# The gates of the last five tiles of the last unit, projected behind all projections

## The chip, the core and the metric

One NeuronCore of one Trainium2 chip runs the whole program in one launch. The metric is the device time in microseconds, the median over runs; the profile is one execution taken by the hardware profiler. TensorE multiplies (PE in the rows; its weight loads are PEld), VectorE is DVE, ScalarE is ACT, GpSimd is POOL, and SyncE (SP) issues the DMAs from one queue, in order.

## What is computed

One layer of a streaming encoder: 2048 prompt rows of 1024 columns and 8 running streams of 16 new rows each with 512 cached keys. A row is normalised, modulated, projected to queries, keys, values, a SiLU path and gates, goes through two attention branches, and is merged:

```python
h, gate = adaln_modulate(xp, c_prompt, norm_g[l], w_ada[l], b_ada[l])
qa, ka, va, za, qb, kb, vb, zb, ga, gb = project_inputs(h, w_in[l], pos_p)   # h @ w_in, split
...
log_1m = jnp.where(mask, jax.nn.log_sigmoid(-z), 0.0)                        # stick-breaking branch
log_a = jax.nn.log_sigmoid(z) + lax.cumsum(log_1m, axis=3, reverse=True) - log_1m
a = jnp.where(mask, jnp.exp(log_a), 0.0)
...
ya = (oa.reshape(b, s, WIDTH_A) * jax.nn.silu(za)) @ w_branch_a
yb = (ob.reshape(b, s, WIDTH_B) * jax.nn.silu(zb)) @ w_branch_b
return (jax.nn.sigmoid(ga) * ya + jax.nn.sigmoid(gb) * yb) @ w_out
```

The change touches `ga` and `gb`, the 2048 gate columns: they are a part of `h @ w_in` that no attention needs, only the merge at the end.

## The kernel before

**Tiles and units.** The prompt is cut into 16 tiles of 128 rows (t = 0 to 15), the 8 x 16 sample rows are tile 16 (`NT`). The attention is cut into 8 units: units 0, 2, 4, 6 are a head of the differential branch, units 1, 3, 5, 7 two heads of the stick-breaking branch. `steps` is the list of all (unit, tile), the sample tile first in each unit: 136 steps.

**Projection.** `project` makes 12 pieces for a step: 24 matmuls of 128x512 (three products of halves in f16 over eight k) into a PSUM bank `ps_mm`, and in the twelfth piece `finish`, which scales and splits queries, keys and values. Its left operand is the tile of h, 512 KB, which `fetch_h` loads into one of three buffers `hs` (L437), a step ahead. In units 1, 3, 5 and 7, 12 gate pieces follow, two matmuls each (L536), with the unit's 512 gate columns; they go into the single bank `ps_t`, which transposes of queries and keys use too. The last one has ScalarE scale the bank into `gt` (L539), and SyncE stores that to `g_d` in DRAM (L540).

**Attention of unit 7.** For a tile t and each of two heads, chunks of 512 keys: two score matmuls into one of three banks `ps_s` (L696, L697, and L700 with a mask for the diagonal chunk, which comes first), two sigmoids on ScalarE (L130), a scan on VectorE (L670) into `sc_n`. When a segment of up to 8 blocks is scanned, GpSimd multiplies (L676), ScalarE rounds to f16 (L604), VectorE takes the rest (L607), and SyncE transposes both halves by DMA into `wt` (L614). After a lag TensorE sums values with these weights (L757, L758), a pair of matmuls for each half and block.

**Order.** The list `line` holds all projection pieces in order of steps. In turn n of the main loop the attention of step n is interleaved with as many pieces as bring `line` to `position(len(steps) * past / whole + LEAD)`, that is about five steps ahead, by estimated durations. When `line` is used up, the remaining turns take pieces of `early_work` instead: the last of the branch weights, `rest` (buffers for the gates' rows), and the first two tiles of the output stage, whose inputs o and z go into the `hs` buffers 0 and 1 and whose u goes into 2. A scheduler then places every engine's instructions by its own estimates of time; those passed to `kept` stay in program order among each other.

**Output stage.** For each tile: loads of o, z and gate rows, sigmoids, halves of u into `hs` 2 (L314), transposes (L1280), branch matmuls (L1463), transposes of y, output matmuls (L1492); beside it the attention of the sample tile, whose cached keys and values (`dks`, `dc`) are loaded there.

Of the kernel before, what the change touches and what calls it, by code (L numbers as in the profile page):

```python
# [21 lines left out]
AF = mybir.ActivationFunctionType  # L22
# [6 lines left out]
KT = D // P  # L29
# [4 lines left out]
NT = SEQ // P  # L34
# [23 lines left out]
H_AT = 2  # L58
Q_BUFS = 6
TR_AFTER = 5  # L60
LEAD = 5.0
TILE_TIME = 0.6
SAMPLE_TIME = 0.3

GATES = [(u // 2 * 512, u % 2 * 512) for u in range(8)]
# [55 lines left out]
def layer_kernel(ctx: ExitStack, tc: tile.TileContext, a: dict):  # L121
    nc = tc.nc
    V, S, G, T = nc.vector, nc.scalar, nc.gpsimd, nc.tensor
# [12 lines left out]
    def kept(x):  # L136
        tc.keep_in_program_order(x)
        return x
# [190 lines left out]
    units = [None] * 8  # L329
# [101 lines left out]
    silu_z = {}  # L431
    at_hand, ahead, fetched = {}, {}, []

    def fetch_h(u, t):
        ahead[u, t] = hs[len(fetched) % 3].bitcast(F16).rearrange("p (f k n) -> p f k n", f=2, n=P)
        fetched.append(t)
        load(out=ahead[u, t], in_=hT_d[t // 4][:, t % 4, :, :, :])  # L437

    def project(U, t):

        kind, h, sc, sq = U["kind"], U["h"], U["sc"], U["sq"]
        g, i = t // 4, t % 4
        box = {}
# [13 lines left out]
        def mm(n):  # L457
            hi, wi = ((0, 0), (0, 1), (1, 0))[n % 3]
            k = n // 3
            T.matmul(box["p"], box["h"][:, hi, k, :], U["w"][k][:, wi, :], start=(n == 0), stop=(n == 3 * KT - 1))  # L460

        def piece(n):
            if n == 0:
                start()
            for j in range(2 * n, 2 * n + 2):
                mm(j)
            if n == 11:
                finish()
# [57 lines left out]
        g0, gw = GATES[U["u"]]  # L526
        per = 1024 // gw if gw else 0

        def gate_piece(n):

            if n == 0:
                box["g"] = bank("t")
            for j in range(per * n, per * n + per):
                hi, wi = ((0, 0), (0, 1), (1, 0))[j % 3]
                k = j // 3
                T.matmul(box["g"][:, 0:gw], box["h"][:, hi, k, :], U["wg"][k // per][:, k % per, wi, :], start=(j == 0), stop=(j == 3 * KT - 1))  # L536
            if per * n + per == 3 * KT:
                gt = gts[:, 0:512]
                S.activation(out=gt[:, 0:gw], in_=box["g"][:, 0:gw], func=AF.Identity, scale=sc[:, 6:7])  # L539
                load(out=g_d[t][:, g0 : g0 + gw], in_=gt[:, 0:gw])  # L540

        return [lambda n=n: piece(n) for n in range(12)] + [lambda n=n: gate_piece(n) for n in range(3 * KT // per if gw else 0)]

    def transpose_qk(U, t):
        g, i = t // 4, t % 4
# [417 lines left out]
    steps = [(u, t) for u in range(8) for t in [NT] + list(range(NT))]  # L963
# [12 lines left out]
    def projection(m):  # L976
        u, t = steps[m]
        made = []

        def piece(i):  # L980
            if i == 0:
                begin(u, t)
                made.extend(project(units[u], t))
            if i == H_AT and not at_hand and m + 1 < len(steps) and steps[m + 1] not in ahead:
                fetch_h(*steps[m + 1])
            made[i]()

        return [lambda i=i: piece(i) for i in range(12 + 3 * GATES[u][1] // 128)]

    starts = []  # L990
    for m in range(len(steps)):
        starts.append(len(line))
        for i, fn in enumerate(projection(m)):
            line.append((m, fn))
            if i == TR_AFTER and m > 0:
                line.append((m - 1, lambda m=m: transpose_qk(units[steps[m - 1][0]], steps[m - 1][1])))
# [267 lines left out]
    cuts = None  # L1264
    branch_weights = list(range(8))

    L = {}

    def cut(dst, st, src, k, j, s, n):

# [12 lines left out]
    def inputs(t):  # L1283
# [9 lines left out]
        def gates():  # L1293
            gs = []
            for j in range(2):
                gs.append(L["g"][(2 * len(begun) + j) % 4].rearrange("p (b n) -> p b n", b=2))
                load(out=gs[j], in_=g_d[t].rearrange("p (b n) -> p b n", b=2)[:, :, j * 512 : (j + 1) * 512])
            begun.append(t)
            st.update(g=gs, u=L["u"][len(begun) % 2])

# [65 lines left out]
    def early_work():  # L1366


        free.extend(units[7]["bufs"])

        def first(t):
            if "orms" not in L:
                L["orms"] = rsqrt(osums[:, 0:NT, :].rearrange("p t h -> p (t h)"), 4 * NT, P, con, "orms")
            states[t], stages = inputs(t)
            for stage in stages:
                stage()
            if t == tiles[0]:
                turned(states[t])
                opened(states[t])

        def rest():
            L["g"], L["u"], (L["y"], L["y16"]) = free[0:4], free[4:6], free[6:8]

        return [branch_weight for _ in branch_weights] + [rest] + [lambda t=t: first(t) for t in tiles[0:2]]

    for n in range(len(steps) + 2):
        made, qk, side = [], [], []
        if n < len(steps):
            u, t = steps[n]
            past += duration(t)  # L1390
            if t == (3 if u == 0 else NT) and u < 7:
                back += prepare_unit(u + 1)
            if u == 7 and not back and not spare and not cached and len(branch_weights) > 1:
                side.append((1.0, branch_weight))
            for fn in back[: -(-len(back) // max(1, (W_READY if u else W_READY + 2) - t % NT))]:
                side.append((1.0, back.pop(0)))
            for todo, here in ((spare, norm_at), (cached, keys_at)):
                if todo and here(u, t):
                    left = sum(here(*step) for step in steps[n:])
                    for _ in todo[: -(-len(todo) // left)]:  # L1400
                        side.append((1.0, todo.pop(0)))
            if t < NT:
                qk = scores(units[u], t, made)
        target = position(len(steps) * past / whole + LEAD)
        pieces = take(target, min(n + 1, len(steps) - 1))
        if at[0] == len(line) and not pieces and not spare and not cached:
            if cuts is None:
                cuts = early_work()
            pieces = [(1.0, fn) for fn in cuts[: -(-len(cuts) // (len(steps) + 2 - n))]]
            del cuts[: len(pieces)]  # L1410
            if n == len(steps) + 1:
                while due and due[0][2] == 0.0:
                    due.pop(0)[3]()
                pieces += [(PV_B / PIECE, fn) for _, _, _, fn in due]
                due.clear()
        give(interleaved(pieces, qk, side), (PIECE, CHUNK, 0.0))
# [162 lines left out]
```

## Time and profile before

| what | us |
|---|---|
| median of 3 runs (2241.89 to 2244.5) | 2243.91 |
| the profiled execution | 2241.2 |
| its span, first to last instruction | 2239.4 |
| TensorE busy, share of the span | 2082.9, 93% |
| VectorE busy | 1749.2, 78% |
| ScalarE busy | 1621.5, 72% |
| last gate store of unit 7 issued (L540) | 1717.5 |
| last scan of the attention starts (L670) | 1764.2 |
| first branch matmul (L1463) | 1778.8 |

The page gives an engine's busy time and 40 slices of the span with its busy tenths; the table of windows gives the same for stretches that one chooses, with the mean clock granted to TensorE (PEclk) and the share of time in which the DMA engines were busy. In a row of the timeline stand the start, the duration, engine, line, operation, output<-input and, in brackets, the idle time before it with what ended it. Matmuls are pipelined, so the step from one to the next is read from their starts.

### The profile page before, as it was taken

What the parts mean: (1) busy time and instruction counts of PE and PEld (TensorE: products, weight loads), DVE (VectorE), ACT (ScalarE), POOL (GpSimd) and SP (SyncE); (2) the same over time, 40 slices, a digit from 0 to 9 for tenths busy, and PEclk for the clock granted to TensorE, in tenths of its full rate; (3) what the DMA queues carried; (4) which work ended last, traced back from release to release, by engine and by line L of the source; (5) the groups of instructions that cost most, each with busy time, mean ns of one, the idle gap of its engine ahead of it and who ended that gap; (6) DMA issues with size and microseconds to landing.
All of it is one profiled execution on the core that took longest, in us unless ns stands there. A gap on an engine that the chain in (4) does not pass through costs nothing.

```text
span 2239.4 us, 41736 instructions
## 1 busy us (share of the span) xinstructions
PE 2082.9 (93%) x14752; PEld 1127.2 (50%) x14752; DVE 1749.2 (78%) x3795; ACT 1621.5 (72%) x3228; POOL 704.0 (31%) x610
## 2 busy tenths in 40 slices
PE   5998999999999999999989998999998679999997
PEld 3654555555555555555555554555554334444543
DVE  4657868889886788988778888886688868788863
ACT  3967877789877677988677788866677665766641
POOL 1123014456410443742034365402234412212211
PEclk7999999999999999999999999999998799999999
DMA  9777668889796989979879899666677899999521
GB/s 331 266 238 184 165 152 212 196 221 205 197 247 160 224 201 201 213 205 225 200 197 211 182 234 223 170 157 136 140 157 158 183 259 255 235 255 240 158 101 57
DMA packets 805827, 445.30 MB, mean 199 GB/s; under 512 B 537354, under 2 KB 744506, under 8 KB 805104
## 3 DMA queue, kind: packets, MB, share of 16 engines
q1 hardware_dynamic: 804668, 442.24, 79.6%
q8 instruction: 115, 1.88, 0.3%
q14 instruction: 96, 0.79, 0.1%
q10 hardware_dynamic: 948, 0.39, 0.1%
HBM read 228.82 MB, written 86.02 MB: 141 GB/s over the span
## 4 chain that ended last, share of the span: by engine, by line
PE 31%; DVE 7%; ACT 5%; DMA 5%; issue 3%; POOL 1%; SPq 0%; DVEq 0%; POOLq 0%; ACTq 0%
PE ps_o L1492 7%; PE ps_mm L1463 7%; PE ps_mm L460 5%; PE ps_t L536 5%; DMA wt<-sc_n 2%; DVE sc_n L670 2%; PE ps_s L1280 1%; PE ps_s L697 1%; PE ps_s L696 1%; ACT sc_p L130 1%; POOL sc_p L676 1%; PE ps_o L757 1%; PE ps_t L871 1%; ACT sc_n L130 1%; DVE sc_n L607 1%
## 5 line engine op out<-in xcount | busy, mean ns | idle before, releaser
L676 POOL TENSOR_TENSOR sc_p<-sc_p,sc_n 128x127 f32<-128x127 f32 (+7 forms) x192 | 313.1, 1633 | 668.0 <-DVE sc_n L670 515.5
L460 PEld LDWEIGHTS <-hs 128*128 128x128 f16 x3120 | 292.6, 99 | 315.3 <-issue 6.7
L460 PE MATMUL ps_mm<-wa,hs 128*128 128x512 f16 x1590 | 383.3, 380 | 3.3 <-DMA hs<-hT_d 2.1
L460 PE MATMUL ps_mm<-wb,hs 128*128 128x512 f16 x1530 | 382.3, 381 | 0.2 <-DVE qbuf L495 0.2
L536 PE MATMUL ps_t<-wb,hs 128*128 128x512 f16 x1224 | 291.9, 379 | 3.2 <-DVE qst L564 2.9
L670 DVE TENSOR_TENSOR_SCAN sc_n<-ps_s,sc_n,zero_t 128x512 f32<-128x512 f32 x192 | 245.5, 1279 | 35.5 <-ACT ps_s L130 30.1
L696 PE MATMUL ps_s<-k,qst 128*128 128x512 f16 (+3 forms) x640 | 225.7, 354 | 33.5 <-DVE sc_n L670 24.8
L607 DVE TENSOR_TENSOR sc_n<-sc_p,sc_n 128x128 f16<-128x128 f32 (+7 forms) x192 | 221.9, 1158 | 40.0 <-ACT sc_n L604 39.5
L536 PEld LDWEIGHTS <-hs 128*128 128x128 f16 x1632 | 154.8, 98 | 182.2 <-DVE qst L564 7.3
L130 ACT ACTIVATE sc_p<-ps_s,usc 128x512 f32<-128x512 f32 (+3 forms) x320 | 202.9, 634 | 37.6 <-PE ps_s L697 23.0
L697 PE MATMUL ps_s<-k,qst 128*128 128x512 f16 (+3 forms) x640 | 226.1, 354 | 0.0
L604 ACT CAST sc_n<-sc_p 128x128 f16<-128x128 f32 (+7 forms) x192 | 154.8, 807 | 64.7 <-POOL sc_p L676 64.0
L130 ACT ACTIVATE ps_s<-ps_s,usc 128x512 f32<-128x512 f32 (+3 forms) x320 | 195.1, 610 | 0.0
L1492 PE MATMUL ps_o<-wo,wb 128*128 128x512 f16 x816 | 186.7, 385 | 0.7 <-ACT wb L1281 0.7
L757 PE MATMUL ps_o<-v,wt 128*128 128x128 f16 x1088 | 136.1, 227 | 21.8 <-DMA wt<-sc_n 21.8
L1500 POOL TENSOR_TENSOR x<-m,x 128x512 f32<-128x512 f32 x34 | 49.9, 1467 | 272.6 <-DVE m L1496 164.9
L590 DVE TENSOR_SCALAR_CACHE_REDUCE sc_p<-ps_s,usc 128x512 f32<-128x512 f32 (+3 forms) x160 | 106.3, 665 | 32.5 <-PE ps_s L697 18.6
L757 PEld LDWEIGHTS <-wt 128*128 128x128 f16 x1088 | 103.6, 102 | 50.0 <-DMA wt<-sc_n 27.0
L758 PE MATMUL ps_o<-v,wt 128*128 128x64 f16 x1088 | 128.6, 199 | 0.0
L1492 PEld LDWEIGHTS <-wb 128*128 128x128 f16 x816 | 79.6, 99 | 97.1 <-issue 4.6
L670 DVE TENSOR_TENSOR_SCAN sc_n<-ps_s,zero_t 128x128 f32<-128x128 f32 (+3 forms) x128 | 104.2, 815 | 22.9 <-ACT ps_s L130 22.1
L501 POOL TENSOR_TENSOR rot<-pr,rope 128x256 f32<-128x256 f32 x68 | 56.8, 835 | 203.8 <-ACT pr L474 115.1
(370 smaller groups left out, 4572.2 us busy)
## 6 DMA issues: line engine op xcount, KB each, us to landing
hs<-hT_d SPq DMA_DIRECT2D x130, 512.0 KB, 4.8
g_d<-gt SPq DMA_DIRECT2D x68, 256.0 KB, 3.1
out_dram<-pr SPq DMA_DIRECT2D x204, 64.0 KB, 3.6
wa<-in_w_in_dram SPq DMA_DIRECT2D x34, 256.0 KB, 5.3
o_d<-o SPq DMA_DIRECT2D x136, 64.0 KB, 2.0
wa<-g_d SPq DMA_DIRECT2D x17, 512.0 KB, 4.7
wb<-g_d SPq DMA_DIRECT2D x17, 512.0 KB, 4.8
hs<-o_d SPq DMA_DIRECT2D x17, 512.0 KB, 4.2
```

Of the source, the lines that this page charges most:

```text
L130: i = S.activation(**kw)
L460: T.matmul(box["p"], box["h"][:, hi, k, :], U["w"][k][:, wi, :], start=(n == 0), stop=(n == 3 * KT - 1))
L536: T.matmul(box["g"][:, 0:gw], box["h"][:, hi, k, :], U["wg"][k // per][:, k % per, wi, :], start=(j == 0), stop=(j == 3 * KT - 1))
L604: x = S.copy(out=hi, in_=src)
L607: V.tensor_tensor(out=lo, in0=src, in1=hi, op=ALU.subtract)
L670: V.tensor_tensor_scan(out=dst[:, lo : lo + n][:, ::-1], data0=src[:, 0:n][:, ::-1], data1=zero_t[:, 0:1].to_broadcast([P, n]), initial=fi ...
L676: G.tensor_tensor(out=p[:, 0:m], in0=p[:, 0:m], in1=n[:, 1 : m + 1], op=ALU.mult)
L696: T.matmul(p[:, 0:n], qst[:, c, :], kk[:, c, 0:n], start=True, stop=False)
L697: T.matmul(p[:, 0:n], qst[:, 2 + c, :], kk[:, c, 0:n], start=False, stop=not diag)
L757: T.matmul(po[:, c * P : (c + 1) * P], wt[:, wj, :], vt[:, c, :, :], start=first, stop=False)
L1463: T.matmul(pb, st["u"][:, ui * 8 + br * 4 + k, :], wb[br * 4 + k // 2 * 2 + j][:, wi, k % 2, :], start=(n == 0), stop=(n == 11))
L1492: T.matmul(po, st["y"][:, yi * 8 + k, :], wo[j * 4 + k // 2][:, wi, k % 2, :], start=(n == 0), stop=(n == 3 * KT - 1))
```

## The change

`late` names the five steps of unit 7 with t = 11 to 15. For them `project` keeps the 12 gate pieces aside and `projection` issues the first 12 pieces alone, so `line` is 60 pieces shorter. `late_gates` makes these 60 pieces again, in the order t = 13, 14, 15, 11, 12 (`behind`). When `line` is used up, turns take from `behind` first, spread over the turns up to the last but one, and `early_work` follows. The tiles 13, 14 and 15 of h are the last three that were loaded and are still in the three `hs` buffers; those of 11 and 12 are loaded a second time, into the buffers of 13 and 14 when their gates are done. The first matmul of each piece and the evacuation are `kept`.

```diff
+LATE, LATE_DONE = 5, 1
...
+    def late(u, t):
+        return u == 7 and NT - LATE <= t < NT
...
-                T.matmul(box["g"][:, 0:gw], box["h"][:, hi, k, :], U["wg"][k // per][:, k % per, wi, :], start=(j == 0), stop=(j == 3 * KT - 1))
+                x = T.matmul(box["g"][:, 0:gw], box["h"][:, hi, k, :], U["wg"][k // per][:, k % per, wi, :], start=(j == 0), stop=(j == 3 * KT - 1))
+                if late(U["u"], t) and j == per * n:
+                    kept(x)
...
-        return [lambda n=n: piece(n) for n in range(12)] + [lambda n=n: gate_piece(n) for n in range(3 * KT // per if gw else 0)]
+        U["gates", t] = box, [lambda n=n: gate_piece(n) for n in range(3 * KT // per if gw else 0)]
+        return [lambda n=n: piece(n) for n in range(12)] + ([] if late(U["u"], t) else U.pop(("gates", t))[1])
...
-        return [lambda i=i: piece(i) for i in range(12 + 3 * GATES[u][1] // 128)]
+        return [lambda i=i: piece(i) for i in range(12 + (0 if late(u, t) else 3 * GATES[u][1] // 128))]
+
+    def late_gates(t):
+
+        def piece(i):
+            box, made = units[7]["gates", t]
+            if i == 0:
+                if t < NT - 3:
+                    box["h"] = ahead[8, t]
+            made[i]()
+            if i == len(made) - 1 and t >= NT - 3 and NT - LATE + t - (NT - 3) < NT - 3:
+                fetch_h(8, NT - LATE + t - (NT - 3))
+
+        return [lambda i=i: piece(i) for i in range(3 * GATES[7][1] // 128)]
...
+    behind = [fn for t in list(range(NT - 3, NT)) + list(range(NT - LATE, NT - 3)) for fn in late_gates(t)]
...
-            if cuts is None:
-                cuts = early_work()
-            pieces = [(1.0, fn) for fn in cuts[: -(-len(cuts) // (len(steps) + 2 - n))]]
-            del cuts[: len(pieces)]
+            todo = behind
+            left = max(1, len(steps) - LATE_DONE - n)
+            if not behind:
+                if cuts is None:
+                    cuts = early_work()
+                todo, left = cuts, len(steps) + 2 - n
+            pieces = [(1.0, fn) for fn in todo[: -(-len(todo) // left)]]
+            del todo[: len(pieces)]
```

What becomes of it is seen in the order of the built programs. Line numbers of the changed kernel are higher: L540 is the gate matmul (L536 before), L705 and L706 the scores, L766 and L767 the value sum, L623 the DMA transpose, L441 the load of h, L548 the store of gates.

TensorE at t = 13, before: the last gate (t = 15) ends, the first scores of t = 13 follow (256 columns in `ps_s_21915`), then value sums and scores.

```order
L536 MATMUL ps_t_21835<-wb6_1432,hs0_180 128x512
...
L536 MATMUL ps_t_21835<-wb0_1426,hs0_180 128x512
...
L696 MATMUL ps_s_21915<-k_21461,qst_21630 128x256
...
L757 MATMUL ps_o_21842<-v_20665,wt_21646 128x128
...
L696 MATMUL ps_s_21924<-k_20764,qst_21630 128x512
```

TensorE at the same place in the changed kernel: scores of t = 13 (`ps_s_21768`), value sums, and only then the first late gate, that of t = 13 (`hs1`).

```order
L705 MATMUL ps_s_21768<-k_21395,qst_21519 128x256
...
L705 MATMUL ps_s_21783<-k_20764,qst_21519 128x512
...
L766 MATMUL ps_o_21810<-v_19306,wt_21505 128x128
...
L540 MATMUL ps_t_21765<-wb3_1429,hs1_181 128x512
...
L705 MATMUL ps_s_21799<-k_20082,qst_21519 128x512
...
L540 MATMUL ps_t_21765<-wb0_1426,hs1_181 128x512
```

All five gates now stand between the first scores of t = 13 and the first of t = 15, with the remaining scores of t = 13 and 14 and 138 matmuls of the value sum between them; before, none did.

SyncE in the same part, before: a transpose of t = 12, the last gate store, and loads for the output stage right behind the last of t = 12 (its `wt` has 10 half blocks).

```order
L614 DMA_TRANSPOSE wt_21897<-sc_n_21800 128x10x128
L1297 DMA wb3_1429<-g_d1_97 128x2x512
L1290 DMA hs0_180<-o_d0_62 128x1024
L540 DMA g_d15_111<-gt0_1421 128x512
```

SyncE in the changed kernel: the stores of the late gates, the two reloads of h (`hs1`, `hs2` from `hT_d`) and the first loads of the output stage (o, z, a row of gates) stand between the transposes of t = 13 and 14.

```order
L548 DMA g_d13_109<-gt0_1421 128x512
L441 DMA hs1_181<-hT_d2_59 128x2048
L623 DMA_TRANSPOSE wt_21854<-sc_n_21773 128x12x128
L441 DMA hs2_182<-hT_d3_60 128x2048
...
L1313 DMA hs0_180<-o_d0_62 128x1024
...
L1314 DMA hs1_181<-z_d0_79 128x512
L623 DMA_TRANSPOSE wt_22098<-sc_n_22039 128x16x128
L548 DMA g_d11_107<-gt0_1421 128x512
L1320 DMA wb3_1429<-g_d1_97 128x2x512
```

Each of these loads waits for the gate whose buffer it overwrites, and the transposes that follow it are issued after it.

ScalarE early in the output stage, before (`v16c` is cached values, `dsc` the sample tile's exponentials, `hs2` the halves of u):

```order
L314 ACTIVATE v16c_22923<-dc_22758,s_c_22586 128x8x128
...
L314 ACTIVATE v16c_23051<-dc_22804,s_c_22586 128x8x128
L130 ACT_TABLE_LOAD
L130 ACTIVATE dsc_22865,l_22891<-dsc_22865,nm_22889 128x640
...
L130 ACT_TABLE_LOAD
L130 ACTIVATE hs1_181<-hs1_181 128x512
L314 ACTIVATE hs2_182<-hs0_180,suy_22775 128x1024
```

ScalarE there in the changed kernel:

```order
L315 ACTIVATE wo7_22634<-x_22633,s_w8_19830 128x1024
L131 ACT_TABLE_LOAD
L131 ACTIVATE dsc_22867,l_22893<-dsc_22867,nm_22891 128x640
...
L315 ACTIVATE v16c_23053<-dc_22806,s_c_22588 128x8x128
L1496 CAST wa5_174<-wb3_1429 128x512
L315 ACTIVATE hs2_182<-hs0_180,suy_22777 128x1024
L131 ACT_TABLE_LOAD
L131 ACTIVATE hs1_181<-hs1_181 128x512
```

The table load with the exponentials has moved ahead of the last cached values, and the halves ahead of the second table load; `wo7`, the last of the output weights, stood behind both before. With it, the 48 output matmuls of the first tile (L1492), which stood as 30, 8, 10 with transposes and branch matmuls of the next tiles between, are one row of 48.

More of the change, by code (lines that the diff above doesn't have):

```diff
@@ L535, in gate_piece @@
                 k = j // 3
-                T.matmul(box["g"][:, 0:gw], box["h"][:, hi, k, :], U["wg"][k // per][:, k % per, wi, :], start=(j == 0), stop=(j == 3 * KT - 1))
+                x = T.matmul(box["g"][:, 0:gw], box["h"][:, hi, k, :], U["wg"][k // per][:, k % per, wi, :], start=(j == 0), stop=(j == 3 * KT - 1))
+                if late(U["u"], t) and j == per * n:
+                    kept(x)
             if per * n + per == 3 * KT:
                 gt = gts[:, 0:512]
-                S.activation(out=gt[:, 0:gw], in_=box["g"][:, 0:gw], func=AF.Identity, scale=sc[:, 6:7])
+                x = S.activation(out=gt[:, 0:gw], in_=box["g"][:, 0:gw], func=AF.Identity, scale=sc[:, 6:7])
+                if late(U["u"], t):
+                    kept(x)
                 load(out=g_d[t][:, g0 : g0 + gw], in_=gt[:, 0:gw])
-        return [lambda n=n: piece(n) for n in range(12)] + [lambda n=n: gate_piece(n) for n in range(3 * KT // per if gw else 0)]
+        U["gates", t] = box, [lambda n=n: gate_piece(n) for n in range(3 * KT // per if gw else 0)]
+        return [lambda n=n: piece(n) for n in range(12)] + ([] if late(U["u"], t) else U.pop(("gates", t))[1])
     def transpose_qk(U, t):
```

## The prediction

> **What bounds the kernel now.** I read the page first, for the place where TensorE, nearly full everywhere else, has room:
>
> ```profile
> PE 2082.9 (93%) x14752; PEld 1127.2 (50%) x14752; DVE 1749.2 (78%) x3795; ACT 1621.5 (72%) x3228; POOL 704.0 (31%) x610
> PE   5998999999999999999989998999998679999997
> PEclk7999999999999999999999999999998799999999
> ```
>
> Slices 31 to 33 (about 1680 to 1850 us) are the last attention tiles and the start of the output stage. I cut that part by the table of windows, at the first scan of an attention tile of the last unit (t = 9, 13, 14, 15), at the last scan and at the first branch matmul:
>
> ```profile
> core 0: us, PE busy (x) PEld busy (x) DVE busy (x) ACT busy (x) POOL busy (x), PEclk, DMA share, GB/s
> 1644.10:1716.65 72.55, 72.21 (x514) 38.42 (x512) 57.52 (x85) 55.03 (x109) 25.24 (x20) 1.00 0.75 161
> 1716.65:1731.60 14.95, 9.13 (x76) 5.19 (x75) 14.04 (x20) 12.60 (x24) 9.27 (x6) 0.69 0.67 162
> 1731.60:1748.90 17.30, 11.34 (x75) 6.48 (x75) 16.57 (x18) 13.99 (x24) 10.37 (x5) 0.60 0.67 118
> 1748.90:1765.40 16.50, 7.34 (x73) 4.25 (x72) 16.12 (x17) 12.41 (x19) 10.31 (x5) 0.81 0.71 118
> 1778.80:1827.00 48.20, 36.45 (x208) 16.44 (x208) 35.84 (x77) 27.36 (x35) 10.02 (x7) 0.92 0.99 257
> 1716.65:1765.40 48.75, 27.81 (x222) 15.91 (x220) 46.73 (x53) 39.00 (x64) 29.95 (x16) 0.70 0.68 131
> ```
>
> Up to 1716.65 TensorE is the bound (72.21 of 72.55 us) and VectorE has 15 us to spare. From there to 1765.40 it is the reverse: VectorE 46.73 of 48.75 us (0.958), TensorE 57%, and its granted clock falls to 0.60. So work taken off TensorE in the first stretch is worth something only until VectorE is full there, and what is added in the second costs only what TensorE cannot fit.
>
> **The change, part by part.** It moves 5 gates of 24 matmuls of 128x512. Their price, and that of what stands beside them, is the distance of starts in the timeline of TensorE:
>
> ```profile
> 1709.45 0.22 PE L757 MATMUL ps_o<-v,wt 128*128 128x128 f16 x1
> 1709.54 0.22 PE L757 MATMUL ps_o<-v,wt 128*128 128x128 f16 x1
> 1710.22 1.46 PE L536 MATMUL ps_t<-wa,hs 128*128 128x512 f16 x6
> 1711.52 1.46 PE L536 MATMUL ps_t<-wb,hs 128*128 128x512 f16 x6
> 1714.54 0.27 PE L696 MATMUL ps_s<-k,qst 128*128 128x256 f16 x1
> 1723.62 0.59 PE L696 MATMUL ps_s<-k,qst 128*128 128x512 f16 x1 [1.86 <-DVE sc_n L670]
> 1733.38 0.61 PE L696 MATMUL ps_s<-k,qst 128*128 128x512 f16 x1
> 1733.78 0.63 PE L697 MATMUL ps_s<-k,qst 128*128 128x512 f16 x1
> 1743.79 0.38 PE L696 MATMUL ps_s<-k,qst 128*128 128x512 f16 x1 [0.46 <-DVE sc_n L670]
> ```
>
> Six gate matmuls take 1.30 us, so one 0.216 and 120 of them 25.9 us. A pair of the weighted value sum (L757, L758) takes 0.085 us. At a low clock a 128x512 matmul takes 0.40 us (1733.38 to 1733.78).
>
> *First stretch, t = 9 to 12.* All 120 left from here (in the planner 7, 17, 12 and 24 gate pieces of two matmuls at t = 9 to 12). TensorE's load falls to 72.21 - 25.9 = 46.3 us and VectorE's 57.52 becomes the bound. How full can VectorE get? The second stretch shows 0.958 with TensorE half idle; below stand the two fullest mixed stretches, 0.914 and 0.892, in which TensorE is busy too.
>
> ```profile
> 200.00:300.00 100.00, 86.51 (x629) 49.85 (x628) 80.19 (x219) 76.95 (x175) 7.80 (x9) 0.95 0.67 157
> 500.00:600.00 100.00, 96.30 (x730) 53.36 (x729) 91.37 (x194) 88.39 (x191) 58.70 (x56) 1.00 0.89 207
> 700.00:800.00 100.00, 93.58 (x647) 50.98 (x645) 73.50 (x165) 75.05 (x166) 33.66 (x32) 1.00 0.84 206
> 900.00:1000.00 100.00, 93.14 (x711) 52.21 (x709) 89.21 (x190) 88.09 (x190) 61.28 (x57) 0.98 0.91 210
> ```
>
> 57.52 / 0.958 = 60.0 and 57.52 / 0.892 = 64.5 us are the ends. I take 0.935, between them since TensorE's load will be between those of the rows: 61.5 us, a gain of **11.0** (8.1 to 12.5).
>
> That TensorE will have holes here brings its clock in. At 61% busy the clock was 0.69, at 87% 0.95; 46.3 us at about 0.85 are 54 us, still under 61.5, and this is why I don't take 0.958. [...]
>
> *Second stretch, t = 13 and 14.* In the new order all 120 gate matmuls stand between the first scores of t = 13 and the first of t = 15. Before, this took TensorE 1743.79 - 1714.54 = 29.25 us, with idle time and at the low clock. Now it holds 25.9 us of gates; 12 pairs of 512-column scores, 12 x 2 x 0.216 = 5.2; four shorter pairs with their masks, 1.3; 69 pairs of the value sum, 5.9: 38.3 us at full clock. That exceeds the 32.3 us which VectorE takes for these two tiles (1716.65 to 1748.90), so **TensorE becomes the bound here**. It will be 38.3 of some 41 us busy, 93%, and at 93 to 96% the rows above show a clock of 0.98 to 1.00, so full clock stands. To it come stalls behind the weight transposes. These are what SyncE's rows and TensorE's waits show now:
>
> ```profile
> 1746.30 0.29 PE L757 MATMUL ps_o<-v,wt 128*128 128x128 f16 x1 [1.86 <-DMA wt<-sc_n]
> 1752.02 0.23 PE L757 MATMUL ps_o<-v,wt 128*128 128x128 f16 x1 [1.13 <-DMA wt<-sc_n]
> 1741.23 12.29 SPq L614 DMA_TRANSPOSE wt<-sc_n  x4
> hs<-hT_d SPq DMA_DIRECT2D x130, 512.0 KB, 4.8
> ```
>
> I take 3 us of stalls (two such waits), with 1 and 6 as ends: 41.3 us. The lead of TensorE over the scan matters too:
>
> ```profile
> 1716.65 0.69 DVE L670 TENSOR_TENSOR_SCAN sc_n<-ps_s,zero_t 128x256 f32<-128x256 f32 x1
> 1748.94 1.21 DVE L670 TENSOR_TENSOR_SCAN sc_n<-ps_s,zero_t 128x512 f32<-128x512 f32 x1
> ```
>
> Before, scores led the scan by 2.1 us at t = 13 (TensorE the bound) and 5.15 us at t = 15 (VectorE the bound). Afterwards it should be the other way round, 5.15 and 2.1. So scan to scan the stretch takes 41.3 - 5.15 + 2.1 = 38.3 us instead of 32.3: a loss of **6.0** (4.0 to 9.0).
>
> *Waits that are added.* SyncE's queue now holds the two reloads of h, which wait for the gates of t = 13 and 14, and the first loads of the output stage (o, z and one of the gates' rows), which wait for the gates of t = 15, 11 and 12; the transposes of tiles 13 and 14 queue behind them, and TensorE's value sums wait for those. A reload itself lands in 4.8 us, and between its issue and its use stand two gates (10.4 us) and other matmuls, so it costs nothing unless the queue stands. ScalarE evacuates the five gates here instead of earlier:
>
> ```profile
> L539 ACT ACTIVATE gt<-ps_t,usc x10: 687/687/719, 1596.2 to 1715.2; 128x512 f32<-128x512 f32 x10
> ```
>
> Five times 0.69 is 3.4 us; 39.00 + 3.4 of 38.3 + 16.5 = 54.8 us is no bound. A gate also waits for the evacuation of the one before, since its PSUM bank is single; between two gates stand 1.5 us or more of other matmuls.
>
> *Tile 15 and the end of attention* hold no gate and stay at 16.5 + 13.4 us.
>
> *Output stage.* The scheduler has also reordered its beginning, where TensorE stood 11.75 of 48.20 us:
>
> ```profile
> 1812.11 6.64 PE L1492 MATMUL ps_o<-wo,wb 128*128 128x512 f16 x30
> 1826.03 1.03 PE L1280 MATMUL ps_s<-id,hs 128*128 128x128 f16 x8 [7.28 <-ACT hs L314]
> 1818.29 1.15 ACT L314 ACTIVATE v16c<-dc,s_c 128x1024 f16<-128x1024 f32 x1 [0.52 <-DMA dc<-in_cache_a_v_dram]
> 1819.46 1.28 ACT L130 ACT_TABLE_LOAD   x1
> 1823.01 1.28 ACT L130 ACT_TABLE_LOAD   x1
> 1824.84 1.13 ACT L314 ACTIVATE hs<-hs,suy 128x1024 f16<-128x1024 f32 x1
> ```
>
> In the new order the halves of hs stand ahead of the second table load, and the first load with its two exponentials ahead of the last two v16c: of 6.5 us between 1818.29 and 1824.84 only v16c (1.15) and a short cast stay, so some 4.7 leave the path. And all 48 output matmuls of the tile stand ahead of the stall, not 30, so 18 x 0.216 = 3.9 us more of it is filled. Against it, DMA is 0.99 busy here, and the last load of the output weights now goes ahead of the caches'. Ends: 6 us gained; 4 us lost (one landing more on the path). I take a gain of **1.5**, since saturated DMA will give much of it back.
>
> *Sum*: -11.0 + 6.0 - 1.5 = -6.5 us on a span of 2239.4 (execution 2241.2), so 2232.9 (2234.7). That execution lies 2.7 us under the median of 2243.9; I predict a median of **2237.4 us**. The ends together give -14.5 to +4.9.
>
> **Rivals.** *All hidden (15%)*: VectorE as full as in the second stretch now, 12.5 gained, 4 lost, and the output stage gives 5: 13.5, 2230.4 us. For it: the transposes hardly stopped TensorE in the first stretch. Against: three engines near full at once.
>
> *Given back (25%)*: TensorE's work is only shifted, and with VectorE at 0.90 and 5 us of stalls the tail is 8.6 gained, 8 lost, the output stage nothing: 2243.3 us. For it: the second stretch's load (38.3) exceeds its room.
>
> *The SyncE queue stands (13%, slower)*: the five added waits each hold the transposes behind them some 2.5 us too long (the size of the waits for wt above, 1.13 and 1.86, plus an issue), TensorE halts at the value sums that stand ahead of the next gate, and that gate frees the next load later. 12.5 us of stalls beyond the 3 make it +7.5 in the tail, with nothing from the output stage 2251.4 us. It decides from 8 us of stalls in the second stretch on. Against it: loads were issued between transposes before, too, without such a halt.
>
> *Cold gates (5%, slower)*: if the clock stays where it is now in this stretch, 120 matmuls take 0.40 instead of 0.216 us, 22 us more, some 2259 us. The rows at 93% speak against it.
>
> **Chances.** Forecast 42%. This kernel's measurement tells 0.2% (4.5 us) from no change, so up to 2239.4 is faster: forecast and "all hidden", 57%; "given back" is the same, 25%; slower 18%. Range 2231 to 2246: it leaves out the far end of "all hidden" and the two slower rivals; the forecast's own is 2232 to 2239.
>
> **What would show it.** Right: gates of t = 11 to 15 beside the scores of t = 13 and 14 at 0.216 us each; the first scan of t = 13 about 11 us earlier, that of t = 15 about 5, TensorE over 90% busy between, and VectorE no longer. Wrong: waits for wt of more than 6 us in that stretch; a clock under 0.9 there; a stretch t = 9 to 12 above 65 us; or an output stage that is longer from first branch matmul to the end.

## The result, and the profile after

The changed kernel takes 2237.2 us (median of 22 runs, 2232.59 to 2244.71) against 2243.8 us for the kernel before in the same comparison (22 runs, 2235.05 to 2250.03): a ratio of 0.9971, 95% interval 0.9961 to 0.9981. Two more comparisons on other occasions gave 0.9959 (0.9948 to 0.9971) and 0.9976 (0.9963 to 0.999). So it is some 5 to 9 us faster, 0.3%.

From the page of the changed kernel, the span, the busy times and the 40 slices of TensorE and its clock:

```profile
span 2233.3 us, 41751 instructions
PE 2074.0 (93%) x14752; PEld 1123.6 (50%) x14752; DVE 1749.3 (78%) x3795; ACT 1621.4 (73%) x3228; POOL 699.5 (31%) x610
PE   5998899999999999999999998999898699999997
PEclk7999999999999999999999999999999799999999
```

The dip of slices 31 to 33 before (8, 6 and 7 tenths) has lost its last slice; the share of busy TensorE is 93% as before. For the rest I use the same cuts as the prediction, and name them: **A** from the first scan of t = 9 to the first of t = 13, **B** from there to the first of t = 15, then t = 15 up to the *start* of the last scan, the end of the attention up to the first branch matmul, and the **output stage** to the end of the span. The table of windows of the changed kernel, five rows in this order (length first, then busy time and count of each engine, clock, DMA share):

```profile
core 0: us, PE busy (x) PEld busy (x) DVE busy (x) ACT busy (x) POOL busy (x), PEclk, DMA share, GB/s
1648.50:1706.52 58.02, 50.26 (x399) 28.40 (x398) 53.96 (x85) 52.45 (x106) 24.34 (x19) 0.94 0.83 168
1706.52:1748.93 42.41, 40.23 (x294) 21.34 (x293) 31.83 (x36) 27.48 (x47) 19.66 (x12) 0.97 0.81 186
1748.93:1764.46 15.53, 6.15 (x45) 3.19 (x44) 14.97 (x17) 12.88 (x20) 9.85 (x4) 0.77 0.49 101
1764.46:1779.44 14.98, 7.56 (x80) 6.67 (x81) 9.07 (x26) 7.71 (x12) 5.43 (x5) 0.50 0.97 225
1779.44:2233.30 453.86, 430.62 (x3076) 211.21 (x3076) 338.52 (x762) 260.25 (x355) 86.53 (x62) 0.98 0.74 199
```

The same five of the kernel before:

```profile
1644.13:1716.65 72.52, 72.18 (x513) 38.42 (x512) 57.52 (x85) 55.01 (x109) 25.24 (x20) 1.00 0.75 161
1716.65:1748.94 32.29, 20.51 (x150) 11.70 (x149) 30.65 (x38) 26.63 (x46) 19.64 (x11) 0.64 0.67 138
1748.94:1764.15 15.21, 7.30 (x73) 4.21 (x72) 14.83 (x15) 12.03 (x19) 10.31 (x5) 0.84 0.74 121
1764.15:1778.82 14.67, 7.54 (x80) 6.65 (x81) 9.08 (x26) 8.09 (x13) 5.16 (x5) 0.50 0.95 226
1778.82:2239.40 460.58, 431.89 (x3076) 210.57 (x3076) 336.94 (x762) 260.23 (x355) 89.51 (x62) 0.97 0.73 196
```

A went from 72.5 to 58.0 (-14.5), B from 32.3 to 42.4 (+10.1); the next two grew by 0.3 each; the output stage gave 6.7 in this pair of executions. The roles are swapped as forecast: in A VectorE is now busy 0.93 of the time and TensorE 0.87; in B TensorE is busy 40.23 of 42.41 us. Note that the first scan of t = 9 comes 4.4 us *later* than before: executions of one kernel differ there by more than that (1644.13 and 1654.20 in two profiles of the kernel before). So stretches are compared from this scan on, not spans.

### The profile page after: what moved, and what is told of

Same layout as the page of the kernel before. It is cut to its first block, busy times and chain, and to the rows that moved or that the text cites. A ratio compares the mean times of both kernels' runs of the same rounds, so it can differ in the third digit from the quotient of the medians.

```text
span 2233.3 us, 41751 instructions
## 1 busy us (share of the span) xinstructions
PE 2074.0 (93%) x14752; PEld 1123.6 (50%) x14752; DVE 1749.3 (78%) x3795; ACT 1621.4 (73%) x3228; POOL 699.5 (31%) x610
## 5 line engine op out<-in xcount | busy, mean ns | idle before, releaser
L685 POOL TENSOR_TENSOR sc_p<-sc_p,sc_n 128x127 f32<-128x127 f32 (+7 forms) x192 | 310.7, 1622 | 673.1 <-DVE sc_n L679 526.1
L540 PE MATMUL ps_t<-wb,hs 128*128 128x512 f16 x1224 | 293.3, 380 | 3.5 <-DVE qst L573 2.9
L705 PE MATMUL ps_s<-k,qst 128*128 128x512 f16 (+3 forms) x640 | 223.6, 350 | 34.7 <-DVE sc_n L679 27.4
L616 DVE TENSOR_TENSOR sc_n<-sc_p,sc_n 128x128 f16<-128x128 f32 (+7 forms) x192 | 218.8, 1143 | 42.7 <-ACT sc_n L613 42.2
L540 PEld LDWEIGHTS <-hs 128*128 128x128 f16 x1632 | 154.8, 98 | 182.6 <-DVE qst L573 7.3
L706 PE MATMUL ps_s<-k,qst 128*128 128x512 f16 (+3 forms) x640 | 223.7, 350 | 0.0
L766 PE MATMUL ps_o<-v,wt 128*128 128x128 f16 x1088 | 135.9, 226 | 22.8 <-DMA wt<-sc_n 22.6
L767 PE MATMUL ps_o<-v,wt 128*128 128x64 f16 x1088 | 127.9, 198 | 0.0
L766 PEld LDWEIGHTS <-wt 128*128 128x128 f16 x1088 | 102.4, 101 | 50.7 <-DMA wt<-sc_n 26.8
L505 POOL TENSOR_TENSOR rot<-pr,rope 128x256 f32<-128x256 f32 x68 | 58.2, 856 | 201.3 <-ACT pr L478 131.1
L762 PE MATMUL ps_o<-v,wt 128*128 128x128 f16 x544 | 101.6, 224 | 21.0 <-DMA wt<-sc_n 20.8
```

The lines of the kernel that those rows point to most:

```text
L540: x = T.matmul(box["g"][:, 0:gw], box["h"][:, hi, k, :], U["wg"][k // per][:, k % per, wi, :], start=(j == 0), stop=(j == 3 * KT - 1))
L616: V.tensor_tensor(out=lo, in0=src, in1=hi, op=ALU.subtract)
L685: G.tensor_tensor(out=p[:, 0:m], in0=p[:, 0:m], in1=n[:, 1 : m + 1], op=ALU.mult)
L705: T.matmul(p[:, 0:n], qst[:, c, :], kk[:, c, 0:n], start=True, stop=False)
L706: T.matmul(p[:, 0:n], qst[:, 2 + c, :], kk[:, c, 0:n], start=False, stop=not diag)
L766: T.matmul(po[:, c * P : (c + 1) * P], wt[:, wj, :], vt[:, c, :, :], start=first, stop=False)
```

## Experiments

The table holds every profiled execution. "Late gates" are the recorded gate matmuls of the late tiles in A, B and t = 15 (120 in all, 24 to a tile; some records are double or missing, and with five late tiles the first two start in the last 0.8 us of A); times in us. A dash stands where there is one execution alone, and so no ratio.

| kernel | late gates A, B, t = 15 | A | B | t = 15 | to branch | output stage | ratio to before (95%) |
|---|---|---|---|---|---|---|---|
| before, twice | 120, 0, 0 | 72.5, 72.5 | 32.3, 32.2 | 15.2, 15.2 | 14.7, 15.0 | 460.6, 460.2 | 1 |
| the change, three times | 0, 119, 0 | 58.0, 58.0, 58.0 | 42.4, 42.4, 42.4 | 15.5, 15.5, 15.5 | 15.0, 15.1, 15.1 | 453.9, 459.5, 459.7 | 0.9971, 0.9959, 0.9976 |
| five late, over t = 13 to 15, twice | 0, 71, 48 | 58.1, 58.0 | 34.3, 35.3 | 18.5, 18.2 | 14.1, 14.0 | 460.1, 461.8 | 0.9957 (0.9941 to 0.9974), 0.9967 (0.9953 to 0.9981) |
| four late, over t = 13 and 14 | 24, 76, 22 | 59.7 | 35.5 | 15.7 | 17.3 | 460.2 | 0.9966 (0.9953 to 0.9979) |
| four late, over t = 13 to 15 | 24, 52, 46 | 59.8 | 34.7 | 14.8 | 16.9 | 461.9 | 0.9969 (0.9956 to 0.9981) |
| three late, over t = 13 and 14 | 48, 72, 0 | 61.3 | 41.7 | 14.3 | 15.5 | 461.2 | 0.9994 (0.998 to 1.0008) |
| three late, over t = 13 to 15 | 48, 48, 24 | 61.3 | 37.1 | 13.5 | 16.8 | 463.6 | 0.996 (0.9947 to 0.9973) |
| five late, 23 of 24 matmuls left out | 0, 5, 0 | 58.0 | 32.9 | 16.3 | 15.1 | 462.4 | 0.994 (0.9919 to 0.996) |
| three late, short products | 48, 72, 0 | 61.3 | 37.5 | 11.2 | 17.0 | 464.3 | - |
| the change, short products | 0, 119, 0 | 58.1 | 40.6 | 16.2 | 14.8 | 458.8 | - |

The theory: B's length is set by TensorE, which the gates fill, and A's by VectorE. The rivals: the place of the gates in the order, not their amount; VectorE's own stretched operations; the output stage's new order as the real source of the gain.

**Three late tiles instead of five**, none loaded twice:

```diff
-LATE, LATE_DONE = 5, 1
+LATE, LATE_DONE = 3, 1
```

> Three late tiles in place of five (the gates of t=13, 14 and 15 alone stand behind the projections, all from the h at hand, none loaded twice). The stretches are A (first scan of t=9 to first scan of t=13; 72.5 us before, 58.0 with the change), B (to the first scan of t=15; 32.3 and 42.4) and the output stage (its first matmul to the end; 460.6 and 453.9). Theory T (in B TensorE has become the bound, by the number of gate matmuls put there): 48 matmuls of 0.216 us leave B and come back to A. B's TensorE work falls from 40.2 to about 30 us, under VectorE's 31 to 32, so B is 32 to 35; A's TensorE work rises from 50.3 to about 60.7, so A is 60 to 63; A and B together 93 to 98 against 100.4 with the change and 104.8 before, and the kernel 3 to 7 us faster than with the change if the output stage stays. Rival R (it is not the amount but the order: blocks of up to 24 gates stand ahead of the score matmuls on TensorE and each makes the next scan late by its own length): two blocks less of five, so B falls only by what stood ahead of scores, to 38 or more. Rival O (the gain is the output stage's new order and nothing of the gates): A and B together stay within 3 us of 100.4 or of 104.8, and the time follows the output stage.

Measured: no gain at all (0.9994). A is 61.3 as expected, but B is 41.7, not 32 to 35, although only 72 gates stand in it. The theory in its plain form falls here: TensorE is busy 33.1 of B's 41.7 us. The window row shows who is full instead, VectorE with 37.84:

```profile
1715.75:1757.44 41.69, 33.11 (x254) 18.55 (x252) 37.84 (x39) 30.58 (x52) 20.04 (x11) 0.92 0.75 159
```

Its groups of instructions in B (busy time, mean, and idle time before), the subtraction L616 (in the expectations also called a sum) ahead of all others:

```profile
L616 DVE TENSOR_TENSOR sc_n<-sc_p,sc_n 128x1024 f16<-128x1024 f32 (+3 forms) x9 | 17.0, 1896 | 0.0
L679 DVE TENSOR_TENSOR_SCAN sc_n<-ps_s,sc_n,zero_t 128x512 f32<-128x512 f32 x12 | 15.4, 1280 | 1.0 <-ACT ps_s L131 0.3
L240 DVE TENSOR_SCALAR sc_q<-ps_t 128x8 f32<-128x8 f32 x1 | 0.2, 167 | 2.0 <-PE ps_t L232 2.0
```

The twelve scans of 512 columns take 1.280 us each, against 1.279 in the changed kernel's B and 1.280 in that of before. Nine subtractions take 17.0 us; in the changed kernel nine took 12.6. The timelines of GpSimd and VectorE in this run show how one of them is stretched:

```profile
1739.37 1.77 POOL L685 TENSOR_TENSOR sc_p<-sc_p,sc_n 128x895 f32<-128x895 f32 x1 [2.02 <-DVE sc_n L679]
1739.40 2.82 DVE L616 TENSOR_TENSOR sc_n<-sc_p,sc_n 128x1024 f16<-128x1024 f32 x1
```

and an undisturbed one in the changed kernel:

```profile
1720.43 1.23 DVE L616 TENSOR_TENSOR sc_n<-sc_p,sc_n 128x1024 f16<-128x1024 f32 x1 [2.67 <-ACT sc_n L613]
```

The product ends at 1741.14 and the subtraction, started 0.03 us after it, at 1742.22, 1.08 us after the product's end. The undisturbed one takes 1.23 us in all, so this one got next to nothing done beside the product.

**Five late tiles, spread over three tiles of attention instead of two**:

```diff
-LATE, LATE_DONE = 5, 1
+LATE, LATE_DONE = 5, 0
```

> Five late tiles, but their 60 pieces are spread over the tiles t=13, 14 and 15 instead of 13 and 14, so that about 80 of 120 gate matmuls stand in B and about 40 beside t=15's scans (C, first to last scan of t=15, 15.5 us with the change, of which TensorE works 6.2). Theory T: B's TensorE work falls from 40.2 by about 8.6 us to some 32, so B is 32 to 36; C takes 8.6 us of gates into 9 us of idle TensorE and stays 15 to 18; A is the 58 of the change. The tail is 5 to 9 us shorter than with the change, the kernel 4 to 9 us faster. Rival R (each block of gates makes the score behind it late by its own length, idle TensorE or not): what B loses C takes on, C 22 to 25, no gain over the change within 2 us.

Measured: B 34.3, A 58.1 and the tail to the first branch matmul 124.9 against 130.9 us, as the theory had it, 0.9957. What B lost is not all free: t = 15 grew by 3 us to 18.5, half a microsecond over the 15 to 18 that was expected, and TensorE is busy 17.50 of 18.46 us there. The rows of B and of t = 15:

```profile
1716.82:1751.15 34.33, 27.35 (x219) 14.92 (x218) 31.99 (x35) 26.49 (x45) 19.43 (x11) 1.00 0.85 178
1751.15:1769.61 18.46, 17.50 (x120) 9.08 (x117) 13.71 (x13) 12.53 (x20) 10.35 (x6) 0.91 0.77 156
```

**Four late tiles** (`LATE, LATE_DONE = 4, 1`):

> Four late tiles (t=12 to 15), one h loaded twice, over t=13 and 14. Theory T: 24 matmuls (5.2 us) leave B and come back to A: B 36 to 39, A 58 to 60, the two 95 to 98 against 100.4 with the change, the kernel 2 to 5 us faster if the output stage stays at 453.9. Rival R: B 40 to 42, A 58 to 60, no gain over the change. Rival O: no change of A and B together beyond 3 us; the output stage, whose order has again one row of 48 output matmuls as with the change, is again near 454.

Measured: A 59.7, B 35.5, 0.9966. The two together are 95.2, within the theory's 95 to 98; in time it is not to be told from the change. B lies under the expected 36 to 39, since 22 gates fell into t = 15 as well. The output stage takes 460.2 us. Its row of 48 output matmuls is not the change's: it stands 3.55 us for output weights after the first 30, where the change's runs through, so this run does not test rival O.

**Three late tiles over three** (`LATE, LATE_DONE = 3, 0`):

> Three late tiles, spread over t=13, 14 and 15: about 48 gate matmuls in B, 24 beside t=15. Theory T: B's TensorE work is about 20.5 + 10.4 = 30.9 less a few us that the change had brought from A, under VectorE's 31 to 32: B 32 to 34, A 60 to 63, C 15 to 17; the tail as with three late tiles over two tiles, or up to 2 us better. Rival R: C rises by 5 us. Rival O: its output stage has the order of before (30, 8 and 10 output matmuls apart, and no row of 48), so the stage is again near 460, 5 to 7 us over the change's 453.9; if the order does not matter it is within 3 us of 454.

Measured: A 61.3, t = 15 13.5, but B 37.1, over the 32 to 34 that the theory gave; TensorE waits 5.4 us for scans and 4.8 for transposed weights there, and VectorE is busy 33.23. What holds B here was not settled. The timed ratio, 0.996, is better than its stretches give.

**The changed kernel again**, unedited:

> The changed kernel again, unedited, for what repeats of its stretches. First profile, from the first scan of t=9: A 58.0, B 42.4, t=15 15.5, last scan to first matmul of the output stage 15.0, output stage 453.9 (before: 72.5, 32.3, 15.2, 14.7, 460.6). If the output stage's 6.7 us less belong to the change, it is again within 2 us of 454 and the kernel 0.5% faster or more; if they are one execution's chance, it is 457 to 461 and the ratio 0.997 to 0.998, the tail alone.

Measured: A, B and t = 15 the same to 0.1 us. The output stage is 459.5, and 459.7 in a third profile; with the same order of instructions in all three, the first profile's 453.9 was that execution's chance. Ratio 0.9959, which is 9.2 us, while the stretches up to the first branch matmul give 3.9; where the rest comes from was not found.

**The kernel before again**, unedited:

> The kernel before again, unedited: its output stage was 460.6 us in the first profile, with 17.2 us of idle TensorE. If the order of the instructions sets it, it is 459 to 462 again; if it is chance, anywhere from 454 to 464. A and B, with no run-to-run choice, 72 to 73 and 32 to 33.

Measured: 460.2 and the same stretches; A 72.5, B 32.2.

**The late gates left out**: of each late tile's 24 gate matmuls only the first is issued.

```diff
+                if late(U["u"], t) and j > 0:
+                    continue
-... stop=(j == 3 * KT - 1))
+... stop=(j == 3 * KT - 1 or late(U["u"], t)))
```

> The changed kernel with all but the first gate matmul of each of the five late tiles left out (their gates are not the reference's; loads, evacuations and stores stay). Theory T (B's 42.4 us are set by TensorE, which the 120 gates fill): without them VectorE is the bound, as before: B 31 to 34, A 57 to 59, t=15 15 to 16, so the tail is 8 to 11 us shorter than with the change. Rival V (VectorE's sums, stretched beside GpSimd's products, set B: 12.6 us of sums with the change, 17.0 with three late tiles, 10.6 before): which sums are stretched hangs on the order, so B stays at 37 or more. Output stage: its order is that of the run with three late tiles over three tiles (463.6 us there); if order sets it, 461 to 465; if not, anywhere.

Measured: B 32.9, although its subtractions take 13.0 us and not less than the 12.6 of the change, so theory T holds and rival V falls for the changed kernel: with the gates on TensorE its B is 9.5 us longer. (The scheduler's order differs a little between the two, so the 9.5 us are not the matmuls' alone to the last microsecond.) The row of B:

```profile
1708.56:1741.46 32.90, 20.43 (x161) 11.41 (x160) 31.76 (x34) 26.89 (x47) 19.21 (x11) 0.80 0.96 210
```

The whole kernel is then 0.6% faster than before (0.994, 0.9919 to 0.996): 13.6 us, between 9 and 18, is what five tiles of gates are worth when they cost almost nothing.

**Four late tiles over three** (`LATE, LATE_DONE = 4, 0`):

> Four late tiles over t=13, 14 and 15. Theory T with the bound of both engines (A, B and t=15 together cannot fall under VectorE's busy time of about 100 us, and were 110.8 to 111.9 for the three mixes that left TensorE room): 109 to 113 for the three together, against 116.0 with the change, so 3 to 7 us faster than it up to the output stage. Rival V: 114 to 118, as with three late tiles over two (117.3). The output stage has the same order as with three late tiles over three: 461 to 465 if order sets it.

Measured: A, B and t = 15 together 109.3 us, in the theory's 109 to 113; the output stage 461.9. Up to the first branch matmul it takes 126.2 us, 4.7 less than the change. The time does not show it: 0.9969, against 0.9959 for the change in the same comparison.

**The products cut**, in the kernel with three late tiles and in the changed one: GpSimd's L685 works on two columns instead of up to 1024 for t = 13 and 14. The scheduler also moves some value sums and scans by it.

```diff
-        m = (seg["hi"] - seg["lo"]) * P - (later is None)
+        m = 2 if job["U"]["u"] == 7 and job["t"] in (13, 14) else (seg["hi"] - seg["lo"]) * P - (later is None)
```

> Three late tiles over t=13 and 14 (B was 41.7 us, TensorE 33.1 and VectorE 37.8 of it busy), with the product on GpSimd of the tiles t=13 and 14 cut to its first two columns (so their attention weights are not the reference's). Theory L (VectorE's L616, the operation that the expectations before call a sum, stands blocked while GpSimd's product runs; 17.0 us for 9 of them against 1.22 us for an undisturbed one of 1024 columns): L616 falls to 9 to 11 us in B and B to 33 to 37. Rival T (gates ahead of scores set B): B stays at 40 or more.

> The same cut of the products in the changed kernel (B 42.4, TensorE 40.2 of it busy). Theory T: TensorE is the bound there, so B stays 40.5 to 42.5 although VectorE's L616 gets shorter (12.6 to about 10 us). If the blocked L616 or the chain scan, product, halves, subtraction set B here too, it falls under 39.

Measured with three late tiles: the subtractions fall from 17.0 to 10.7 us and B from 41.7 to 37.5, half a microsecond over the range of theory L and well under the rival's 40. In the changed kernel they fall from 12.6 to 11.2 and B only from 42.4 to 40.6, as TensorE's 39.56 us allow. The L616 row and the row of B, three late tiles:

```profile
L616 DVE TENSOR_TENSOR sc_n<-sc_p,sc_n 128x1024 f16<-128x1024 f32 (+3 forms) x9 | 10.7, 1201 | 2.1 <-ACT sc_n L613 2.1
...
1716.03:1753.51 37.48, 32.14 (x261) 18.09 (x258) 31.35 (x42) 29.59 (x51) 6.80 (x11) 0.96 0.83 173
```

and the changed kernel:

```profile
1713.83:1754.47 40.64, 39.56 (x292) 21.10 (x291) 30.66 (x36) 28.05 (x47) 8.35 (x12) 0.97 0.95 201
```

So one edit takes 4.2 us where VectorE was the fuller engine and 1.8 where TensorE was, as it should if the same stretch has another bound in each. These are single profiles. In the kernel with three late tiles the products shorten the chain before the subtraction as well, so the 4.2 us are not the shorter subtractions alone.

**Five late tiles over three, beside the changed kernel on one chip**, the two most alike:

> Five late tiles over t=13, 14 and 15 again, beside the changed kernel on the same chip. Its tail from the first scan of t=9 to the first matmul of the output stage was 124.9 us against 130.9 with the change: if the stretches repeat (58.0, 34.3, 18.5, 14.1) and the output stages are the same but for chance, it is 4 to 8 us (0.2 to 0.35%) faster than the change. If the tail's gain is given back in the output stage, the two are within 0.1%.

> The changed kernel a third time: A 58.0, B 42.4 and t=15 15.5 as twice before. Output stage 453.9 and 459.5 before; a third value between them or near 459 makes the first one the chance, near 454 the second. Time 0.3 to 0.4% under the kernel before.

Measured: 2243.85 us (0.9967) against 2245.63 (0.9976, 0.9963 to 0.999). The tail repeats, 125.5 against 131.1 us; the output stage takes 461.8 against 459.7, of which about one, by an estimate from the stretch before it (1.1 us shorter), is 18 matmuls that in this order stand behind the first branch matmul (3094 matmuls in it, not 3076). The expected 4 to 8 us over the change were not measured: 1.8 us between the medians, with intervals that overlap. It is no worse than the change, and not shown to be better.

## Why the prediction came out right, step by step

**The total.** Forecast -6.5 us and a median of 2237.4, with a range of 2231 to 2246; measured 2237.2. Over three profiles of the change and two of before the stretches sum to -14.5 + 10.2 + 0.3 + 0.2 - 2.7 = -6.5 us, and the timed differences are -6.6, -9.2 and -5.3. Up to the first branch matmul the profiles agree on -3.8 us; the other 1.5 to 5.4 us lie in the output stage or ahead of A, where executions of one kernel differ by more than that, and were not traced. That the total fits so well is luck: A and B both came out beyond their own ends, each larger than its figure, by 3.5 and 4.1 us, with opposite signs. Of the signs of being wrong none showed: the waits for wt are 1.2 us, the mean clock in B is 0.97, and A is 58 us.

**A (forecast -11.0, ends -8.1 to -12.5; measured -14.5).** The mechanism is right: VectorE took over as the bound, at a share of 53.96 / 58.02 = 0.930 where 0.935 was chosen. The term that was mis-sized is VectorE's 57.52 us, taken over from before as if fixed. The groups of A before and after:

```profile
L607 DVE TENSOR_TENSOR sc_n<-sc_p,sc_n 128x1024 f16<-128x1024 f32 (+4 forms) x16 | 18.6, 1164 | 6.8 <-ACT sc_n L604 6.7
```

```profile
L616 DVE TENSOR_TENSOR sc_n<-sc_p,sc_n 128x1024 f16<-128x1024 f32 (+4 forms) x15 | 15.5, 1037 | 1.2 <-ACT sc_n L613 1.1
```

These means mix sizes. By size, the eight subtractions of 1024 columns went from 12.1 to 10.0 us, and the two of 384 from 2.7 to 1.1. One subtraction fewer falls into the window (0.8 us when undisturbed), and the others stand less behind products. The timelines of GpSimd and VectorE before show one that does, and one of its size that does not:

```profile
1665.62 2.00 POOL L676 TENSOR_TENSOR sc_p<-sc_p,sc_n 128x1024 f32<-128x1024 f32 x1 [2.66 <-DVE sc_n L670]
1665.90 2.13 DVE L607 TENSOR_TENSOR sc_n<-sc_p,sc_n 128x384 f16<-128x384 f32 x1
1673.65 0.55 DVE L607 TENSOR_TENSOR sc_n<-sc_p,sc_n 128x384 f16<-128x384 f32 x1
```

Four of the 16 stood so before, 3.9 us longer in all than undisturbed ones of their size; with the change it is two of 15, and 1.7 us. No run tried this for A by itself. The runs add what a term of one number cannot show, A by late gates that stay in it: 58.0 (none), 59.7 (24), 61.3 (48), 72.5 (120). The first 72 that leave are worth 0.156 us each, the last 48 only 0.069: VectorE's share goes from 0.87 to 0.93 there.

**B (forecast +6.0, ends 4.0 to 9.0; measured +10.1).** TensorE did become the bound (without the gates B is 32.9), at 0.95. The mean clock in B, 0.97, is near the 0.98 to 1.00 of the prediction, but the step that failed is "so full clock stands": it does not stand where B begins. The timeline of TensorE and the windows of the changed kernel where A passes into B, with the first scores of t = 15 (the mask behind them marks the first chunk):

```profile
1701.95 0.37 PE L705 MATMUL ps_s<-k,qst 128*128 128x256 f16 x1 [2.70 <-DVE sc_n L679]
1703.63 0.58 PE L705 MATMUL ps_s<-k,qst 128*128 128x512 f16 x1 [0.78 <-DVE sc_n L679]
1705.74 2.75 PE L540 MATMUL ps_t<-wb,hs 128*128 128x512 f16 x6
1708.28 2.01 PE L540 MATMUL ps_t<-wa,hs 128*128 128x512 f16 x6
1710.13 1.46 PE L540 MATMUL ps_t<-wb,hs 128*128 128x512 f16 x6
...
1746.86 0.38 PE L705 MATMUL ps_s<-k,qst 128*128 128x512 f16 x1
1747.08 0.38 PE L706 MATMUL ps_s<-k,qst 128*128 128x512 f16 x1
1747.29 0.22 PE L709 MATMUL ps_s<-masks,idb 128*128 128x128 bf16 x1
```

```profile
1698.00:1702.00 4.00, 0.76 (x5) 0.40 (x5) 4.00 (x5) 2.79 (x5) 2.02 (x1) 0.64 0.90 201
1702.00:1706.00 4.00, 3.22 (x24) 2.23 (x24) 3.90 (x7) 3.19 (x8) 1.32 (x1) 0.50 0.45 84
1706.00:1710.00 4.00, 4.00 (x12) 1.46 (x11) 4.00 (x5) 1.38 (x2) 2.00 (x1) 0.58 0.70 131
1710.00:1715.00 5.00, 5.00 (x46) 2.95 (x45) 5.00 (x6) 2.84 (x5) 2.94 (x2) 1.00 0.39 79
```

The same in steps of half a microsecond, where the clock falls and where it rises:

```profile
1698.50:1699.00 0.50, 0.45 (x3) 0.21 (x3) 0.50 (x1) 0.34 (x1) 0.50 (x1) 1.00 0.55 191
1699.00:1699.50 0.50, 0.25 (x3) 0.13 (x2) 0.50 (x1) 0.00 (x0) 0.50 (x1) 0.65 0.19 50
1699.50:1700.00 0.50, 0.00 (x0) 0.00 (x0) 0.50 (x1) 0.00 (x0) 0.50 (x1) 0.50 1.07 214
...
1709.00:1709.50 0.50, 0.50 (x3) 0.17 (x2) 0.50 (x2) 0.50 (x1) 0.00 (x0) 0.61 0.02 2
```

At the end of A TensorE has little to do and waits for scans, since VectorE is the bound there now. Its clock falls to 0.50 at about 1699.2, and at that time TensorE has not yet begun its longest idle time, the 2.70 us from 1699.25 on; the clock is back at about 1709.4. So the first 12 gates take 2.54 + 1.85 us from start to start instead of 2 x 1.30: 1.8 us more. The scores and value sums between 1701.95 and 1705.74 take 3.8 us instead of some 1.5 at the prediction's prices; of these 2.3 us, 0.8 are a wait for a scan and 1.5 the clock. The waits in B are smaller than the 3 us that the prediction put in:

```profile
PE ps_o L766 <- DMA wt<-sc_n: 1.2, 1, 1.2
PE ps_t L540 <- ACT gt L545: 0.6, 1, 0.6
PE ps_s L705 <- DVE sc_n L679: 0.3, 1, 0.3
```

From the first scores of t = 13 (1701.95) to those of t = 15 (1746.86) TensorE needs 44.91 us, 3.6 more than the 41.3 forecast. The slow start accounts for 2.3 + 1.8 us, the waits give back 0.9, and some 0.4 us stay unassigned; there was no long stall. The two leads of TensorE over the scan, forecast at 5.15 and 2.1 us, came out as 4.6 and 2.1, which adds the last half microsecond of the 4.1.

**t = 15 and the end of the attention (forecast 0; measured +0.3 and +0.2).** Right.

**The output stage (forecast -1.5, ends -6 to +4; measured -6.7, and by two later profiles -1.1 and -0.9 against 460.6).** The stall that was named did shrink, from 7.28 us to 3.07, 3.07 and 3.06 in the three profiles of the change:

```profile
1825.16 0.82 PE L1303 MATMUL ps_s<-id,hs 128*128 128x128 f16 x8 [3.07 <-DVE hs L320]
```

In its second execution TensorE then stands longer at the sample tile's transposes:

```profile
1836.93 1.04 PE L1303 MATMUL ps_s<-id,hs 128*128 128x128 f16 x8 [3.07 <-DVE hs L320]
...
1886.98 0.24 PE L880 MATMUL ps_t<-v16c,dwt 128*32 128x128 f16 x4 [3.46 <-DMA dwt<-dsc]
```

The size that was forecast, a gain of 1.5, held in two executions of three. That saturated DMA (0.99 busy in the prediction's row from 1778.80 on) gives the rest back, as the prediction has it, is not shown: which of the later waits does it each time was not followed to the end of the stage.

**The rivals.** *SyncE's queue stands* did not happen in the change: 1.2 us of waits for wt in B, fewer than the 1.9 before. With three late tiles they were 6.5, and there the gain was gone; but VectorE was the fuller engine, so those waits are not shown to be the cause. *Cold gates* came true for 12 of 120 matmuls, 4.39 us instead of 2.60. *All hidden* did not come, and the run without the late gates shows how much it would be: 13.6 us, with a B of 32.9. *Given back* is the nearest to what happened in B (10.1 of 14.5 us given back), and was outweighed by what A gained beyond its figure.

## What to carry to other kernels

When work is moved off the engine that bounds a stretch, the gain ends where the next engine is full, and the last pieces that are moved can cost more where they land than they earn: here the last 48 gate matmuls earn 3.3 us in A, while A, B and t = 15 together took 111.9, 109.3 and 110.8 us with three, four and five late tiles over three tiles of attention. Do not carry the second engine's busy time over as a constant: part of it was standing beside another engine's products (3.9 of VectorE's 57.52 us in A before, 1.7 of 53.96 with the change), and changes with the order. And take a stretch's length from the same landmarks in two executions of each kernel before a few microseconds are given a cause; the 6.7 us of the output stage were mostly one execution's chance.

## What the runs showed of the hardware

The granted clock of TensorE fell to 0.50 at about 1699.2 in the changed kernel, when no gap of TensorE in the 5 us before had been longer than 1.04 us; it was busy 1.95 us in the last 4.00. The gap of 2.70 us came after the fall. The clock stood at full again at about 1709.4, some 10 us later, after almost 6 us of work without a gap. In the kernel before, it fell at about 1722.4, some 0.6 us into the gap of 1.86 us that stands in the prediction's rows, and the longest gap in the 5 us ahead of that one was 1.25 us. So neither fall had a gap of more than 1.25 us in those 5 us; what brings the clock down was not shown.

Where VectorE's subtraction and GpSimd's product met in the rows above, the subtraction stood: it took 2.82 us beside a product, and ended 1.08 us after it, against 1.23 us alone. With the products cut to two columns and three late tiles, nine subtractions took 10.7 us instead of 17.0. What the two operations share was not shown. The product can be the one that stands: in the kernel before, one of 639 columns that started at 1709.08, 0.04 us after a subtraction, took 2.35 us, against 1.31 for the one of this size at 1698.08. Which subtractions meet a product hangs on the order, and so does VectorE's busy time in B: 30.65 us before, 31.83 with the change, 37.84 with three late tiles over two.
